# A macaron layer in split fp32: shifted weight buffers for half-size products, an out-projection in order of readiness, and a root for 1/rms

## The chip, the cores and the metric

The kernel runs on one core of a Trainium2 chip. The metric is the device time of one execution in microseconds (us); several executions of one kernel are given by their median. Matmuls run on TensorE (PE; its weight loads are a row of their own, PEld), elementwise work on VectorE (DVE) and ScalarE (ACT), some on GpSimd (POOL), and transfers are issued by queues, most by SyncE's (SP).

## The reference

One layer on x of 512 tokens by 1024 columns, all in float32:

```python
x = x + 0.5 * swiglu_ffn(rmsnorm(x, ffn1_norm), ffn1_w_gate, ffn1_w_up, ffn1_w_down)
x = x + hybrid_mixer(rmsnorm(x, mix_norm), w_in, q_norm, k_norm, rel_bias, pool_w, pool_scale, w_out)
x = x + 0.5 * swiglu_ffn(rmsnorm(x, ffn2_norm), ffn2_w_gate, ffn2_w_up, ffn2_w_down)
x = rmsnorm(x, final_norm)
```

`swiglu_ffn` is `(silu(x @ gate) * (x @ up)) @ down` with an inner width of 2816. The mixer projects to q, k, v (8 heads of 64) and to u (512 columns); heads attend to all earlier chunks and their own with a relative bias, u goes through trailing means over 2, 4, 8 and 16 tokens and a 128 by 128 map per group. Both results, side by side, go through one out-projection of 1024 by 1024. `rmsnorm` multiplies by 1/sqrt(mean(x*x) + 1e-6).

## The kernel before, in words

**Split products.** Every fp32 matrix is split into a high part (a cast by ACT) and a low part (the rest, by DVE), and a product is three matmuls (`mm3`, L162): high by high, high by low, low by high. The first operand of a matmul is the stationary one, loaded 128 by 128 by PEld; the second streams through.

**Stages.** (1) FFN 1, up: the norm, five of the 22 column blocks in plain form, then 17 blocks in a form with fewer multiplications: the operands are cut in 2 by 2 and seven products of half size are formed (here called half-size up products). For each block `product` (L519) runs seven times, each four steps of `mm3` with 256 streamed columns: 84 matmuls. The stationary operand is a weight part, the streamed one a half of the normed x (`ha`, `xa`, `sa`). (2) FFN 1, down: seven products with 512 streamed columns, in which the weights stream (`Down.product`, L740). (3) The mixer. (4) and (5): FFN 2, up and down. The final norm is folded into the end of stage 5.

**Where weight parts lie.** `part_tiles` (L145) hands out a high and a low tile of 128 by 1024 floats from four places in turn: three in the pool "weights" and one in the pool of the FFN. In the half-size products `high` (L429) takes such a pair for each of four parts of a block, `high11`, `high13`, `high24` and `high22`, always in this order, so that each kind of part always has the same place. Pools lie one behind the other in the memory, in the order in which they are made, and tiles in steps of 32 bytes. In the FFN stages every operand of these products starts at the same remainder of 512 bytes. In the mixer, the tiles `m` (q, k, attention results, pooled results) lie behind one tile `u` and two tiles `us` of 528 floats, 2112 bytes each, and so start 3 x 64 = 192 bytes off that remainder.

**1/rms.** `Norm.per_token` (L279) sums squares with 1-column matmuls and computes 1/sqrt on DVE from an integer guess and three Newton steps (`rsqrt`, L236: 11 operations, with a copy behind them). The end has its own form for one column (`rsqrt_column`, L216). Silu and Exp on ACT each need a table that a load brings in.

**The mixer's order** is written out by a planner at build time: each piece of work is a generator with a rank, and `run_parts` takes, at each simulated PE time, the ranked first one that is ready; `on` adds assumed costs. The order so found is fixed for PE, DVE, ACT and POOL. `products` (L1313) is the lowest rank: q/k, u and v projections, then the out-projection (`project_out`, L1266) in a fixed order of weight chunks: for output blocks 0 to 3 the pooled half, then the attention half by pairs of heads, then blocks 4 to 7. A chunk's product waits until its own source is there. Weights are split two chunks ahead (`next_weights`, L938).

**The end.** The last product of stage 5 is split: output rows 256 to 383 first (`tt` 0), then rows 384 to 511 in two halves of 256 columns. After each come `residual` (DVE), `settle` (squares with a sum on ACT or DVE, and a multiplication by the final gain on POOL) and `finish` (1/rms, scaling, one store of 512 KB per 128 rows).

**Loads of x.** During stage 2 each product from the fifth on issues one load of x (256 KB) on SP's queue, ahead of the next weights.

Of the kernel before, what the change touches and what calls it, by code (L numbers as in the profile page):

```python
# [16 lines left out]
P = 128  # L17
D = 1024
S = 512
# [16 lines left out]
HILO = 3  # L36
PLAIN = 5
PROBS = 3
M_TILES = 18
# [5 lines left out]
SLACK = 2.5  # L45

@with_exitstack
def layer(
# [42 lines left out]
    n_tiles = [0]  # L91

# [77 lines left out]
    def cut(pair, lo, n):  # L170
        return pair[0][:, lo : lo + n], pair[1][:, lo : lo + n]
# [14 lines left out]
    table = const.tile([P, 1], F32, name="table")  # L186
    nc.vector.memset(ones, 1.0)

    nc.scalar.copy(table, ones[:, 0:1])
# [26 lines left out]
    def rsqrt_column(v):  # L216

        half = small.tile([P, 1], F32, tag="rc", name=name("half"), bufs=8)
        y = small.tile([P, 1], F32, tag="rc", name=name("y"), bufs=8)
        neg = small.tile([P, 1], F32, tag="rc", name=name("neg"), bufs=8)  # L220
        nc.vector.tensor_scalar(
            half.bitcast(I32), v.bitcast(I32), 1, None, op0=ALU.logical_shift_right
        )
        nc.vector.tensor_scalar(neg, v, -0.5, None, op0=ALU.mult)
        nc.vector.tensor_scalar(
            y.bitcast(I32), half.bitcast(I32), -1.0, MAGIC, op0=ALU.mult, op1=ALU.add
        )
        for _ in range(3):
            b = small.tile([P, 1], F32, tag="rc", name=name("b"), bufs=8)
            z = small.tile([P, 1], F32, tag="rc", name=name("z"), bufs=8)  # L230
            nc.vector.scalar_tensor_tensor(b, y, neg, y, op0=ALU.mult, op1=ALU.mult)
            nc.vector.scalar_tensor_tensor(z, b, 1.5, y, op0=ALU.add, op1=ALU.mult)
            y = z
        return y

    def rsqrt(v, n):  # L236
# [17 lines left out]
        return y  # L254

    class Norm:
# [22 lines left out]
        def per_token(self, total):  # L279
# [5 lines left out]
            v = small.tile([P, NT], F32, tag="v", name=name("v"))  # L285
            nc.vector.tensor_scalar(v, total[:, :NT], 1.0 / D, EPS, op0=ALU.mult, op1=ALU.add)
            r = rsqrt(v, NT)
            self.r = small.tile([P, NT], F32, tag="r", name=name("r"))
            nc.vector.tensor_copy(self.r, r)
# [13 lines left out]
        def finish(self):  # L303
            self.per_token(abank())
            self.spread(abank())
# [64 lines left out]
    def ffn_up(norm, wA, down, loaded):  # L370
# [236 lines left out]
    class Down:  # L607
# [36 lines left out]
        def begin(self, pool):  # L644
            self.pool, self.acts = pool, []
            self.raws, self.parts, self.pairs = {}, {}, {}
            self.n_products, self.loads = 0, []
# [137 lines left out]
    with tc.tile_pool(name="act1", bufs=1, reuse_waits="tile") as apool:  # L785
# [4 lines left out]
        with tc.manual_schedule(engines={mybir.EngineType.SP}):  # L790
            for g in range(G):
# [53 lines left out]
    with tc.tile_pool(name="mix", bufs=1, reuse_waits="tile") as mpool:  # L845
# [16 lines left out]
        def start(part, rank):  # L862
# [36 lines left out]
        def t_act(n):  # L899
            return 0.18 + n / 1200  # L900

        def t_dve(n):
            return 0.08 + n / 930
# [24 lines left out]
        def prepare():  # L928
            i = len(ready)
            hi = wpool.tile([P, 1024], F32R, tag="hi", name=name("whi"))  # L930
            lo = wpool.tile([P, 1024], F32R, tag="lo", name=name("wlo"))
# [6 lines left out]
        def next_weights(ahead=2):  # L938
            used[0] += 1
            while len(ready) < min(used[0] + ahead, len(sources)):  # L940
                prepare()
                fetch()
            hi, lo, t = ready[used[0] - 1]
# [55 lines left out]
        def project_qk(half):  # L999
# [13 lines left out]
            start(qk_norm(half, raw), RANK_QK)  # L1013
            yield from project(acc, evacuate)

        def qk_norm(half, raw):
# [20 lines left out]
            rs = rsqrt(var.rearrange("p t h -> p (t h)"), NT * 8)  # L1037
            on("dve", 13 * 0.21)
# [67 lines left out]
        def scores(pair):  # L1106
# [7 lines left out]
            for t in range(NT - 1, -1, -1):  # L1114
# [12 lines left out]
                for i, h in enumerate(heads):  # L1127
                    start(softmax(h, t, sc[i], f), RANK_HEAD + 0.01 * h)
# [3 lines left out]
        def head(h):  # L1132
# [19 lines left out]
            for group in ((1, 3), (0,), (2,)):  # L1152
# [13 lines left out]
                start(evacuate(group, at, n, tp, on("pe", n / P * 0.11)), RANK_HEAD + 0.01 * h)  # L1166
# [48 lines left out]
        def pool():  # L1215
            for g in (3, 2, 1, 0):
# [10 lines left out]
                while step < win:  # L1227
                    yield from until(f, "pool")
                    s2 = mpool.tile([P, PAD + S], F32, tag="us", name=name("us"), bufs=2)
                    at = 2 * step - 1  # L1230
                    nc.gpsimd.tensor_tensor(
                        s2[:, at:], s[:, at:], s[:, at - step : PAD + S - step], op=ALU.add
# [6 lines left out]
                    dd, s[:, PAD:], 1.0 / win, u[:, PAD:], op0=ALU.mult, op1=ALU.subtract  # L1239
# [5 lines left out]
                start(pool_map(g, dd, on("dve", t_dve(S) + 0.4)), RANK_POOL)  # L1245
# [20 lines left out]
        def project_out(d0, part, ks, w):  # L1266

            for d in (d0, d0 + 1):
                if d not in out_acc:
                    out_acc[d] = yield from take("mm")  # L1270
            for k in ks:
                if part:
                    while 2 * k + 1 not in done:
                        yield None
                    yield from until(max(done[2 * k], done[2 * k + 1]))
                    src = aT[k]
                else:
                    while pT_out[k] is None:
                        yield None
                    src, f = pT_out[k]  # L1280
# [281 lines left out]
```

## Time and profile before

| what | us |
|---|---|
| median of 3 runs (878.69 to 879.39) | 879.09 |
| the profiled execution | 877.12 |
| its span, first to last instruction | 875.1 |
| PE busy in the span | 856.1 (98%) |
| DVE, ACT, POOL busy | 715.3, 495.7, 126.8 |
| half-size up products, FFN 1 and FFN 2 | 63.6 to 234.2, 588.6 to 758.6 |
| mixer | 346 to 528 |

A matmul's row gives its start and a duration that covers its way through the array; successive matmuls overlap. What a matmul costs in a stream is the distance from its start to the next start (called its pitch here). Where PE is busy without a break, the time of a stage is the number of matmuls times their pitch.

### The profile page before, as it was taken

What the parts mean: (1) busy time and instruction counts of PE and PEld (TensorE: products, weight loads), DVE (VectorE), ACT (ScalarE), POOL (GpSimd) and SP (SyncE); (2) the same over time, 40 slices, a digit from 0 to 9 for tenths busy, and PEclk for the clock granted to TensorE, in tenths of its full rate; (3) what the DMA queues carried; (4) which work ended last, traced back from release to release, by engine and by line L of the source; (5) the groups of instructions that cost most, each with busy time, mean ns of one, the idle gap of its engine ahead of it and who ended that gap; (6) DMA issues with size and microseconds to landing.
All of it is one profiled execution on the core that took longest, in us unless ns stands there. A gap on an engine that the chain in (4) does not pass through costs nothing.

```text
span 875.1 us, 14159 instructions
## 1 busy us (share of the span) xinstructions
PE 856.1 (98%) x5296; PEld 761.5 (87%) x5296; DVE 715.3 (82%) x1151; ACT 495.7 (57%) x841; POOL 126.8 (14%) x209
## 2 busy tenths in 40 slices
PE   9999999999999999989999999999999999999995
PEld 8789999999987888867876787889999999988885
DVE  7799888888887769686777577969888888887897
ACT  7355555555556656548747455445555555556572
POOL 0013112211122000120020000102112111122011
PEclk9999999999999999999999999999999999999998
DMA  8167778768899654222120126247777768899822
GB/s 294 44 193 215 215 226 200 187 193 212 235 326 285 217 200 143 87 85 85 72 73 25 49 97 241 97 119 221 208 228 201 187 197 206 250 326 346 275 91 96
DMA packets 71955, 158.49 MB, mean 181 GB/s; under 512 B 6080, under 2 KB 29136, under 8 KB 71504
## 3 DMA queue, kind: packets, MB, share of 16 engines
q1 hardware_dynamic: 49088, 111.45, 35.4%
q0 software_dynamic: 22656, 46.14, 24.6%
q8 instruction: 41, 0.67, 0.3%
q14 instruction: 26, 0.21, 0.1%
q10 hardware_dynamic: 144, 0.01, 0.0%
HBM read 153.38 MB, written 50.34 MB: 233 GB/s over the span
## 4 chain that ended last, share of the span: by engine, by line
PE 84%; DVE 8%; DMA 4%; ACT 2%; issue 2%; SPq 0%; POOLq 0%; POOL 0%; ACTq 0%; DVEq 0%
PE mm L166 20%; PE mm L167 20%; PE mm L168 20%; PE a L167 6%; PE a L166 6%; PE a L168 6%; DMA raw<-wsum 3%; DVE wlo L124 1%; PE a L1176 1%; PE a L1122 1%; PE a L1164 1%; ACT whi L123 1%; DVE t L1043 1%; DVE aside L324 0%; PE a L192 0%
## 5 line engine op out<-in xcount | busy, mean ns | idle before, releaser
L123 ACT CAST whi<-raw 128x1024 fp32r<-128x1024 f32 (+2 forms) x107 | 102.8, 969 | 72.0 <-PE mm L168 14.6
L124 DVE TENSOR_TENSOR wlo<-raw,whi 128x1024 fp32r<-128x1024 f32 (+2 forms) x107 | 119.5, 1121 | 23.2 <-ACT whi L123 22.6
L168 PE MATMUL mm<-ha,wlo 128*128 128x256 f32 x408 | 115.5, 283 | 0.0
L167 PE MATMUL mm<-ha,whi 128*128 128x256 f32 x408 | 115.5, 283 | 0.0
L166 PE MATMUL mm<-ha,whi 128*128 128x256 f32 x408 | 115.5, 283 | 0.0
L527 ACT ACTIVATE t<-mm 128x256 f32<-128x256 f32 x102 | 39.2, 384 | 125.5 <-PE mm L168 124.8
L436 DVE TENSOR_TENSOR wlo<-wsum,whi 128x1024 fp32r<-128x1024 f32 x68 | 83.0, 1221 | 15.1 <-ACT whi L431 15.1
L167 PEld LDWEIGHTS mm<-ha,whi 128*128 128x128 f32 x408 | 78.3, 192 | 0.1
L166 PEld LDWEIGHTS mm<-ha,whi 128*128 128x128 f32 x408 | 78.3, 192 | 0.1
L168 PEld LDWEIGHTS mm<-ha,wlo 128*128 128x128 f32 x408 | 78.3, 192 | 0.0
L166 PE MATMUL mm<-hhi,whi 128*128 128x512 f32 x192 | 76.8, 403 | 0.7 <-DVE t L382 0.7
L168 PE MATMUL mm<-hhi,wlo 128*128 128x512 f32 x192 | 74.9, 392 | 0.4 <-DVE wlo L124 0.4
L167 PE MATMUL mm<-hlo,whi 128*128 128x512 f32 x192 | 74.9, 391 | 0.0
L660 POOL COPY mark<-t 128x1 f32<-128x1 f32 x40 | 11.7, 291 | 423.3 <-DVE t L572 235.2
L662 POOL DMA_DIRECT2D wsum<-in_wB_dram x72 | 70.1, 1085 | 12.0 <-issue 9.9
L431 ACT CAST whi<-wsum 128x1024 fp32r<-128x1024 f32 x68 | 67.8, 1045 | 4.4 <-PE mm L167 3.9
L167 PE MATMUL mm<-wlo,ah 128*128 128x512 f32 x176 | 68.5, 389 | 0.0
L168 PE MATMUL mm<-whi,ah 128*128 128x512 f32 x176 | 68.5, 389 | 0.0
L166 PE MATMUL mm<-whi,ah 128*128 128x512 f32 x176 | 68.4, 389 | 0.0
L436 DVE TENSOR_TENSOR wlo<-raw,whi 128x512 fp32r<-128x512 f32 x68 | 62.2, 952 | 0.0
L431 ACT CAST whi<-raw 128x512 fp32r<-128x512 f32 x68 | 56.4, 829 | 5.5 <-PE mm L167 4.4
L167 PE MATMUL a<-wlo,ah 128*128 128x512 f32 (+1 forms) x154 | 55.8, 362 | 1.2 <-DVE wlo L124 1.2
(207 smaller groups left out, 2403.2 us busy)
## 6 DMA issues: line engine op xcount, KB each, us to landing
raw<-in_wA_dram SPq DMA_DIRECT2D x87, 512.0 KB, 5.3
wsum<-in_wB_dram POOLq DMA_DIRECT2D x60, 512.0 KB, 6.8
raw<-wsum SPq DMA_DIRECT2D x40, 512.0 KB, 6.1
raw<-in_wB_dram SPq DMA_DIRECT2D x30, 512.0 KB, 5.1
wsum<-wsum POOLq DMA_DIRECT2D x20, 512.0 KB, 5.5
x<-in_xT_dram SPq DMA_DIRECT2D x16, 256.0 KB, 6.0
raw<-in_wQK_dram SPq DMA_DIRECT2D x8, 512.0 KB, 3.5
raw<-in_wO_dram SPq DMA_DIRECT2D x8, 512.0 KB, 3.4
```

What stands on the lines that cost most here:

```text
L123: nc.scalar.copy(hi, src)
L124: nc.vector.tensor_tensor(lo, src, hi.bitcast(F32), op=ALU.subtract)
L166: nc.tensor.matmul(acc, a[0], b[0], start=start, stop=False, **more)
L167: nc.tensor.matmul(acc, a[0], b[1], start=False, stop=False, **more)
L168: nc.tensor.matmul(acc, a[1], b[0], start=False, stop=stop, **more)
L431: nc.scalar.copy(hi, src)
L436: nc.vector.tensor_tensor(lo, src, hi.bitcast(F32), op=ALU.subtract)
L527: nc.scalar.activation(dst, src, AF.Copy, scale=scale)
L660: nc.gpsimd.tensor_copy(mark, after[:, 0:1])
L662: nc.gpsimd.dma_start(self.rows(i, g), self.rows(self.terms[i][at], g), **(dict(accum_op=ALU.add) if at else {}),)
L1043: nc.vector.tensor_tensor(q3, q3, rs[:, t, :].unsqueeze(2).to_broadcast([P, 8, HD]), op=ALU.mult)
L1122: nc.tensor.matmul(sc[i][:, :n], qT[pair][0][a][rows, t * P : (t + 1) * P], kT[pair][0][b][rows, :n], start=a + b == 0, stop=a == 1,)
```

## The change

1. Weight parts lie in buffers of 1152 floats in place of 1024. In the half-size up products the part begins 16, 32, 64 or 8 floats (64, 128, 256 or 32 bytes) into its buffer, by the place; elsewhere at its start.
2. The tiles `us` of the mixer get 40 floats (160 bytes) more each, and a tile `step` of 64 bytes, which nothing uses, is put into the pool "small". The mixer has 16 tiles `m` in place of 18.
3. The out-projection is one generator which takes, among all chunks and sources that are left, the first that is ready at the simulated time; blocks 4 and 5 accumulate in the other group of PSUM banks. Four of its eight weight chunks are split into tiles of the norm's pool.
4. 1/rms of the three norms and of the end: a root on ACT, then reciprocal and one Newton step on DVE (four operations). Loads of the tables for Sqrt and Silu are placed by hand.
5. Loads of x in FFN 1's down stage begin with the 20th product in place of the 5th.
6. The end is written in a fixed order for PE, DVE and ACT: the finishing of rows 256 to 383 stands between the two halves of the last rows, the gain is multiplied on DVE, and the stores of the last two row blocks are split over ACT's and SP's queues.

```diff
-M_TILES = 18
+ROOM, STEPS = 1024 + 128, (16, 32, 64, 8)
+M_TILES = 16
...
+    small.tile([P, 16], F32, name="step", bufs=1)
...
-    def part_tiles():
+    def part_tiles(steps=(0,)):
         pool, bufs = part_rooms[n_parts[0] % len(part_rooms)]
+        at = steps[n_parts[0] % len(steps)]
         n_parts[0] += 1
         return (
-            pool.tile([P, 1024], F32R, tag=tag, name=name("w" + tag), bufs=bufs)
+            pool.tile([P, ROOM], F32R, tag=tag, name=name("w" + tag), bufs=bufs)[:, at : at + 1024]
             for tag in ("hi", "lo")
         )
...
+    def tables(func, after):
+        nc.scalar.activation(table[:, 0:1], after, func, scale=0.0)
+    tables(AF.Sqrt, ones[:, 0:1])
...
+    def rsqrt_of(v, root, out):
+        n = v.shape[-1]
+        y, a, b = (
+            small.tile([P, n], F32, tag=f"rs{n}", name=name("rs"), bufs=3) for _ in range(3)
+        )
+        nc.vector.reciprocal(y, root)
+        nc.vector.tensor_tensor(a, y, y, op=ALU.mult)
+        nc.vector.scalar_tensor_tensor(b, a, -0.5, v, op0=ALU.mult, op1=ALU.mult)
+        nc.vector.scalar_tensor_tensor(out, b, 1.5, y, op0=ALU.add, op1=ALU.mult)
...
+            nc.scalar.activation(root, total[:, :NT], AF.Sqrt, scale=1.0 / D, bias=eps)
+            if after:
+                tables(after, root[:, 0:1])
             nc.vector.tensor_scalar(v, total[:, :NT], 1.0 / D, EPS, op0=ALU.mult, op1=ALU.add)
-            r = rsqrt(v, NT)
+            rsqrt_of(v, root, self.r)
...
-            hi, lo = (z[:, : src.shape[-1]] for z in part_tiles())
+            hi, lo = (z[:, : src.shape[-1]] for z in part_tiles(STEPS))
...
+            if self.n_products == 12:
+                tables(AF.Sqrt, a[0][:, 0, 0:1].bitcast(F32))
-            if self.n_products > 4 and self.loads:
+            if self.n_products > self.loads_from and self.loads:
...
-                    down1.loads = [(x[k], xT[k]) for k in range(KD)]
+                    down1.loads, down1.loads_from = [(x[k], xT[k]) for k in range(KD)], 19
...
-                    s2 = mpool.tile([P, PAD + S], F32, tag="us", name=name("us"), bufs=2)
+                    s2 = mpool.tile([P, PAD + S + 40], F32, tag="us", name=name("us"), bufs=2)
...
+        def project_out():
+            chunks = [(0, 0), (2, 0), (0, 1), (2, 1), (4, 0), (4, 1), (6, 0), (6, 1)]
...
+            while left:
+                times = [start_at(*z) for z in left]
+                at = next((i for i, t in enumerate(times) if t is not None and t <= clock["pe"]), None)
+                if at is None:
+                    yield min((t for t in times if t is not None), default=None)
+                    continue
+                c, k = left.pop(at)
...
+                if len(left) == 16:
+                    tables(AF.Sqrt, ones[:, 0:1])
...
-            if t >= NT // 2:
-                nc.gpsimd.tensor_tensor(z, z, gb[half][:, cols], op=ALU.mult)
+            if t >= NT // 2 and half:
+                nc.vector.tensor_tensor(z, z, gb[half], op=ALU.mult)
...
+                nc.scalar.activation(o[:, S:], xt[NT + t], AF.Copy, scale=r)
+                by_vector(0)
+                nc.scalar.dma_start(rows[:, S:], o[:, S:])
+                nc.sync.dma_start(rows[:, :S], o[:, :S])
...
+        with tc.manual_schedule(engines={E.PE, E.DVE, E.Activation}):
+            for tt in range(2):
+                t = 2 + tt
+                for i, at in enumerate(p7[tt]):
+                    for g, a, w in late:
+                        down2.mms([[at]] * 2, g, a, w, (tt,), further=True)
+                    residual(0, t, *at, scale=-0.5)
+                    if i == 0 and tt:
+                        settle(0, t, 0, *at[1:])
+                        finish(t - 1, mean(t - 1, [1]), 0)
+                        v = mean(t, [1, 0])
+                    else:
+                        settle(0, t, 2 * i, *at[1:])
+            finish(t, v, 2)
```

More of the change, by code (lines that the diff above doesn't have):

```diff
@@ L213, in constants @@
         yield
[L216 to L234, printed above, removed]
     def rsqrt(v, n):
@@ L860, in on, with start @@
             return clock[engine] + HOP
-        def start(part, rank):
+        def start(part, rank, key=None):
+            rank += RANKS.get(key, 0.0)
             n_tiles[0] += 1
@@ L929, in prepare @@
             i = len(ready)
-            hi = wpool.tile([P, 1024], F32R, tag="hi", name=name("whi"))
-            lo = wpool.tile([P, 1024], F32R, tag="lo", name=name("wlo"))
+            if len(sources) - i in (3, 4, 5, 6):
+                hi, lo = (
+                    [hpool.tile([P, S], F32R, tag="h", name=name(what)) for _ in range(2)]
+                    for what in ("whi", "wlo")
+                )
+                for j in range(2):
+                    split(raws[i][:, j * S : (j + 1) * S], hi[j], lo[j])
+                    t = on("dve", t_dve(S), on("act", t_act(S)))
+                ready.append((hi, lo, t))
+                return
+            hi = wpool.tile([P, ROOM], F32R, tag="hi", name=name("whi"))[:, :1024]
+            lo = wpool.tile([P, ROOM], F32R, tag="lo", name=name("wlo"))[:, :1024]
             nc.scalar.copy(hi, raws[i])
@@ L1036, in qk_norm @@
             )
-            rs = rsqrt(var.rearrange("p t h -> p (t h)"), NT * 8)
-            on("dve", 13 * 0.21)
+            v = var.rearrange("p t h -> p (t h)")
+            if half in QK_ROOT:
+                root, rs = (
+                    small.tile([P, NT * 8], F32, tag=what, name=name(what), bufs=1)
+                    for what in ("qk_root", "qk_r")
+                )
+                f = on("dve", 0.4)
+                yield from until(f, "act")
+                nc.scalar.activation(root, v, AF.Sqrt)
+                f = on("act", 0.21)
+                yield from until(f, "dve")
+                rsqrt_of(v, root, rs)
+                on("dve", 4 * 0.21)
+            else:
+                rs = rsqrt(v, NT * 8)
+                on("dve", QK_NORM)
             rs = rs.rearrange("p (t h) -> p t h", h=8)
@@ L1264, in layer, with start_at @@
         out_acc = {}
[L1266 to L1271, printed above, removed]
-                if part:
[L1273 to L1280, printed above, removed]
-                    yield from until(f)
+        def project_out():
+            chunks = [(0, 0), (2, 0), (0, 1), (2, 1), (4, 0), (4, 1), (6, 0), (6, 1)]
+            first = len(sources) - len(chunks)
+            left = [(c, k) for c in range(8) for k in ((0, 1, 2, 3) if chunks[c][1] else (3, 2, 1, 0))]
+            n_left = dict.fromkeys(range(KD), 8)
+            begun = set()
+            def start_at(c, k):
+                d0, part = chunks[c]
+                tag = "a" if d0 == 4 else "mm"
+                if first + c >= len(ready):
+                    return None
+                if d0 not in out_acc:
+                    if len(room[tag]) < 2 or (tag == "a" and len(multiplied) < FILL_AT):
+                        return None
+                t = ready[first + c][2]
+                if d0 not in out_acc:
+                    t = max(t, sorted(room[tag])[1])
+                if part:
+                    if 2 * k + 1 not in done or 2 * k not in done:
+                        return None
+                    return max(t, done[2 * k], done[2 * k + 1])
+                return None if pT_out[k] is None else max(t, pT_out[k][1])
+            prepare_to(len(sources) - len(chunks) + AHEAD)
+            while left:
[5 more added lines that the diff above has]
+                c, k = left.pop(at)
+                d0, part = chunks[c]
+                if c not in begun:
+                    begun.add(c)
+                    prepare_to(first + len(begun) + AHEAD)
+                for d in (d0, d0 + 1):
+                    if d not in out_acc:
+                        tag = "a" if d0 == 4 else "mm"
+                        out_acc[d] = (yield from take(tag)), tag
+                src = aT[k] if part else pT_out[k][0]
@@ L1301, in finish_norm @@
         def finish_norm():
-            while used[0] < 3:
+            while used[0] < NORM_AT:
                 yield None
```

125 lines of the change are left out of this document (61 added, 64 removed).

## Prediction

> **What bounds the kernel now.** First the page: its span, busy times and chain.
>
> ```profile
> span 875.1 us, 14159 instructions
> PE 856.1 (98%) x5296; PEld 761.5 (87%) x5296; DVE 715.3 (82%) x1151; ACT 495.7 (57%) x841; POOL 126.8 (14%) x209
> PE 84%; DVE 8%; DMA 4%; ACT 2%; issue 2%; SPq 0%; POOLq 0%; POOL 0%; ACTq 0%; DVEq 0%
> ```
>
> PE is busy almost throughout and makes the chain. So two things count: the pitch of the matmuls, and the few places where PE stands still. Next the busy times by stage (stretch, its length, then busy time and count for PE, PEld, DVE, ACT, POOL):
>
> ```profile
> 63.60:234.20 170.60, 170.60 (x1422) 170.53 (x1421) 148.50 (x208) 95.07 (x172) 36.35 (x54) 1.00 0.76 201
> 346.00:528.00 182.00, 175.76 (x876) 139.25 (x875) 128.61 (x298) 105.65 (x209) 18.05 (x30) 1.00 0.22 77
> 29.00:31.00 2.00, 1.29 (x6) 0.72 (x6) 1.60 (x3) 1.98 (x3) 0.00 (x0) 1.00 0.00 0
> 279.00:285.00 6.00, 4.79 (x20) 3.35 (x19) 4.83 (x7) 3.88 (x5) 0.00 (x0) 1.00 1.03 297
> 463.00:479.00 16.00, 14.00 (x80) 10.30 (x79) 13.43 (x37) 10.92 (x26) 1.38 (x1) 1.00 0.09 34
> 500.00:504.00 4.00, 2.39 (x12) 1.74 (x11) 1.59 (x3) 0.58 (x1) 0.00 (x0) 1.00 0.00 0
> ```
>
> The half-size products of FFN 1 have no gap: 1422 matmuls in 170.60 us, a pitch of 0.120 us. 512 columns come at 0.227 in the rows below, so 256 columns take 6 ns more than half of that. Nothing but the pitch can shorten this stage. The mixer's PE is idle for 6.2 us; the four short stretches show where PE stands still.
>
> Then the matmuls one by one (start, duration), from FFN 1's down stage and from the out-projection, both with 512 streamed columns:
>
> ```profile
> 239.61 0.39 PE L168 MATMUL mm<-whi,ah 128*128 128x512 f32 x1
> ...
> 242.56 0.39 PE L166 MATMUL mm<-whi,ah 128*128 128x512 f32 x1
> ```
> ```profile
> 504.05 0.40 PE L168 MATMUL mm<-m,wlo 128*128 128x512 f32 x1
> ...
> 506.85 0.40 PE L168 MATMUL mm<-m,wlo 128*128 128x512 f32 x1
> ```
>
> The first are 13 matmuls in 2.95 us, 0.227 each; the second 12 in 2.80 us, 0.2333 each. Shape, clock and split are the same. What differs by the tile sizes is where the operands begin: in the first both at the same remainder of 512 bytes, in the second `m` lies 192 bytes off. **So the place of the operands already costs 6.6 ns per matmul in one stage.**
>
> **The change part by part.** The sum is made against the profiled execution, 877.1 us (its span and 2.0 around it); the median of the runs is 2.0 above that, and I carry these 2.0 over.
>
> *Half-size products (edit 1).* Their number is 2 FFNs x 17 blocks x 84 = 2856, at 0.120. Before, streamed and stationary operand start at the same remainder; after, the weights are shifted: `high11` comes first when ten pairs have been handed out, so by the rotation its part (12 of 84 matmuls) gets 256 bytes, `high13` 32, `high24` 64 and `high22` 128 (24 matmuls each). ACT and DVE, which write the parts, have 75 and 22 us to spare in the stage. What the shift does to the pitch at 256 columns no row shows. The nearest rows are where 256 columns run out of their rhythm, six between matmuls of 512, in the last product:
>
> ```profile
> 852.44 0.28 PE L166 MATMUL a<-whi,ah 128*128 128x256 f32 x1
> ...
> 853.15 0.40 PE L166 MATMUL a<-whi,ah 128*128 128x512 f32 x1
> ...
> 853.85 0.28 PE L166 MATMUL a<-whi,ah 128*128 128x256 f32 x1
> ```
> ```profile
> 862.21 0.28 PE L166 MATMUL a<-whi,ah 128*128 128x256 f32 x1
> 862.32 0.28 PE L167 MATMUL a<-wlo,ah 128*128 128x256 f32 x1
> 862.44 0.28 PE L168 MATMUL a<-whi,ah 128*128 128x256 f32 x1
> ...
> 864.00 0.28 PE L166 MATMUL a<-whi,ah 128*128 128x256 f32 x1
> ```
>
> Six of 256 take 0.71 us, 0.118 each, and the three of 512 behind them 0.70, 0.233 each, just what the off-remainder `m` takes. In an undisturbed row (the second fence) 256 columns begin with 0.11 and settle at 0.120. So there are two regimes: a settled one (0.227 and 0.120) and an unsettled one (0.233 and 0.118), in which 512 columns lose and 256 columns win. The out-projection rows say that a shift gives the unsettled one. Scaled by columns, 0.2333 x 256/512 = 0.1167. I take 0.1175, between 0.1167 and 0.118: -2.5 ns x 2856 = **-7.1 us**. Bounds: half of the settled 512 columns, 0.1135, for all (-18.6), and the out-projection's loss per matmul, +6.6 ns (+18.9). I choose the row with the same 256 columns over the row with the same cause, because what a matmul loses there grows with its columns.
>
> *Tiles `us` and `step` (edit 2).* u and two `us` are now 2112 + 2 x 2272 = 6656 = 13 x 512 bytes, so `m` comes to the common remainder. The small pool, counted tile by tile, stays at 4608 bytes with `step`, and the weights' six buffers add 6 x 512, so everything else keeps its remainder. 192 matmuls of the out-projection and 12 of the pool maps go from 0.2333 to 0.2267: **-1.3 us**. Bounds 0 and -1.4.
>
> *Out-projection as ready (edit 3).* The idle of 2.0 us at 463 and of 1.6 us at 500:
>
> ```profile
> 469.68 0.41 PE L1164 MATMUL a<-ident,prob 128*128 128x128 f32 x2 [0.72 <-DVE m L1191]
> ```
> ```profile
> 501.58 0.50 PE L166 MATMUL mm<-m,whi 128*128 128x512 f32 x1 [0.67 <-ACT m L1186]
> 503.02 0.50 PE L167 MATMUL mm<-m,whi 128*128 128x512 f32 x1 [0.94 <-DVE m L1191]
> ```
>
> At 501.58 PE waits for the last head's result while the pooled halves of blocks 4 to 7, which don't need it, stand behind; the new order has them. At 463 to 479 the first pairs of heads are done and could be used. The wait that may come instead is for weights: a chunk is split by ACT and DVE two chunks ahead, four of the chunks wait for the norm's tiles, free only after the last u product, and 16 tiles `m` in place of 18 must do. I take 3.0 of 3.6: **-3.0 us**. Bounds -3.6 and +2.0 (a stall as long as that at 463 once more). The stall at 375 to 384, behind the q/k norm, keeps its 11-operation root and stays.
>
> *Root (edit 4).* The first norm, and the table load behind it:
>
> ```profile
> 22.74 0.16 DVE L286 TENSOR_SCALAR v<-a 128x4 f32<-128x4 f32 x1 [0.75 <-PE a L281]
> ...
> 26.17 0.17 DVE L289 COPY r<-z 128x4 f32<-128x4 f32 x1
> ```
> ```profile
> 30.15 0.50 PE L166 MATMUL mm<-hhi,whi 128*128 128x512 f32 x1 [0.71 <-DVE t L382]
> ```
> ```profile
> L384 ACT ACT_TABLE_LOAD x2 | 2.6, 1283 | 0.0
> ```
>
> Small DVE operations follow at 0.2 us: 12 behind the first become 4 and a hop to ACT, some 1.3 us less, and the load of Silu's table (1.28) moves in front, into ACT's idle time. The evacuation for which PE waits 0.71 us at 30.15 starts earlier: **-0.7 us** (0 to -1.1). The two other norms lie under PE's work. Three more table loads (about 3.8 us of ACT) lie in stages where ACT has a third of its time free.
>
> *Loads of x (edit 5).* PE stands 1.2 us between 279 and 285, at weights that landed late, after eight loads of 256 KB went ahead on SP's queue. Now these go behind the 19th product, to about 285 to 306, where the DMA engines are as full. **-0.8 us**, bounds -1.2 and +1.2.
>
> *The end (edit 6).*
>
> ```profile
> 864.13 1.30 POOL L1392 TENSOR_TENSOR xt<-xt,t 128x512 f32<-128x512 f32 x1 [20.52 <-ACT t L1388]
> ```
> ```profile
> 864.27 1.17 DVE L1400 SCALAR_TENSOR_TENSOR v<-ssq,v 128x1 f32<-128x1 f32 x1
> ...
> 867.69 0.42 DVE L1375 SCALAR_TENSOR_TENSOR xt<-a,xt 128x256 f32<-128x256 f32 x1
> ```
> ```profile
> 870.65 0.72 ACT L1416 ACTIVATE o<-xt,z 128x512 f32<-128x512 f32 x1 [1.46 <-issue]
> ```
> ```profile
> L1411 DVE SCALAR_TENSOR_TENSOR o<-xt,z,t x4: 746/748/750, 858.4 to 861.9; 128x512 f32<-128x512 f32 x4
> ```
>
> A one-element operation lasts 1.17 us here, as long as POOL's multiplication: those go. The new order, from the first half's end at 864.2: residual 0.4 (864.6), squares 0.6, root 0.3 (865.5), four DVE operations 0.8, scaling 0.75 (867.1), two sums 0.3, the last residual 0.42 (867.8), squares 0.5, root 0.3, four operations 0.8 (869.4), scaling 0.75: 870.2 where the page has 871.4. **-1.1 us**, bounds +0.5 (the store issued by ACT in the way) and -2.0. The cost of the new order is that the last residual stands behind the finishing of the rows before.
>
> *Sum.* Without edit 1: 1.3 + 3.0 + 0.7 + 0.8 + 1.1 = 6.9. With it 14.0: 877.1 - 14.0 = 863.1, and 2.0 for the median: **865 us**.
>
> **The rivals.**
>
> *B: the shift does nothing.* The pitch is 0.120 for whichever of the four places a part lies in, and only 512-column rows have shown an influence; half of the shifts (128, 256) may be too even. Time: 879.1 - 6.9 = 872. The Trainium skill speaks for B: "SBUF — State Buffer", section "Who interferes with whom", gives PE two independent read ports, for streamed operand and weight load, and says that PE never waits on anyone. By that the place could not matter and 872 would follow; the 6.6 ns between the two 512-column rows speak against it.
>
> *C: the shift costs what it costs in the out-projection.* Place: the two half-size stages; price: 6.6 ns per matmul, however many columns. For it speaks that the cause is the same, a difference in remainders, and that all its 204 matmuls lose; against it the 256-column rows. With two of the three large kinds of parts hit (4/7 of 2856) 10.8 us: 872.2 + 10.8 = 883; with all 891. It turns the sign once the mean pitch rises by 6.9/2856 = 2.4 ns, at 37% of the matmuls.
>
> *D: the 6 ns that 256 columns take above half of 512 go,* pitch 0.1135: 872.2 - 18.6 = 854. For it: undisturbed rows of 256 begin with 0.11; against: none stays there.
>
> *E: the mixer's order gains nothing* because weights or tiles `m` come late: 3.0 us lost, A at 868.
>
> **How the numbers follow.** A (unsettled, with E inside its range of 859 to 871) 40%, B 18%, C 32% (875 to 891, mean 883), D 10%. The range from 853 to 885 leaves out about half of D, a quarter of C and the ends of A, 16% in all. About 0.2% (1.8 us) is what a measurement of this kernel can tell from no change. Faster: A, D, 17 of B and 6 of C, 73%; within: 1 of B and 5 of C, 6%; slower: 21 of C.
>
> **What would show it.** The pitch in the half-size stages, separately by part: 0.1175 for A, 0.120 for B, 0.1266 for C, 0.1135 for D; the stage lasts 167, 170.6, up to 180, or 161.5 us. In the out-projection 0.2267. No idle at 500, little at 463. A last scaling that begins 3.5 us after PE's last matmul in place of 4.7. The forecast is wrong if the half-size pitch rises, or if the parts differ in sign.

## The result and the profile after

The changed kernel takes **868.23 us** (median of 4 runs, 865.23 to 869.31) where the kernel before takes 879.24 beside it (878.69 to 879.93): a ratio of 0.9859, with a 95% interval from 0.9824 to 0.9894. The forecast was 865. The profiled execution took 867.31 us, 9.8 less than the one of before.

The page of the changed kernel, its span, busy times and chain:

```profile
span 865.4 us, 14127 instructions
PE 849.9 (98%) x5296; PEld 755.9 (87%) x5296; DVE 708.1 (82%) x1115; ACT 500.9 (58%) x859; POOL 126.9 (15%) x204
PE 89%; DMA 3%; DVE 3%; ACT 2%; issue 1%; SPq 0%; ACTq 0%; DVEq 0%
```

PE has the same 5296 matmuls and is still the bound. Busy time by stage after (stretch, its length, then busy time and count for PE, PEld, DVE, ACT, POOL, granted clock, DMA share, GB/s), and of before the down stage of FFN 1 and the mixer whole:

```profile
62.20:231.60 169.40, 169.40 (x1428) 169.40 (x1427) 148.56 (x207) 95.26 (x172) 36.33 (x54) 1.00 0.78 204
231.70:342.40 110.70, 108.85 (x482) 87.61 (x480) 87.11 (x114) 69.83 (x99) 14.78 (x16) 1.00 0.80 239
342.40:522.00 179.60, 175.17 (x886) 140.24 (x885) 130.21 (x297) 107.65 (x217) 18.06 (x30) 1.00 0.24 80
582.10:751.60 169.50, 169.50 (x1429) 169.49 (x1428) 148.73 (x208) 95.61 (x173) 33.28 (x54) 1.00 0.75 205
463.00:479.00 16.00, 15.92 (x90) 12.72 (x90) 15.42 (x35) 10.40 (x24) 1.38 (x1) 1.00 0.29 100
```
```profile
235.10:343.70 108.60, 107.39 (x480) 87.76 (x480) 87.35 (x114) 68.03 (x97) 12.28 (x16) 1.00 0.79 244
343.80:528.10 184.30, 178.06 (x887) 141.03 (x886) 130.91 (x300) 105.65 (x209) 18.05 (x30) 1.00 0.22 78
```

From these stretches and the starts of the matmuls at their borders, with the differences against before:

| stage | before | after | difference | forecast |
|---|---|---|---|---|
| FFN 1 up: norm and plain blocks | 63.6 | 62.2 | -1.4 | -0.7 |
| FFN 1 and 2: half-size products | 171.5, 171.4 | 169.6, 169.6 | -3.7 | -7.1 |
| FFN 1 down | 108.7 | 110.7 | **+2.0** | -0.8 |
| mixer | 184.3 | 179.6 | -4.7 | -4.3 |
| FFN 2 up: transposes, norm, plain blocks | 60.5 | 60.1 | -0.4 | 0 |
| FFN 2 down | 106.0 | 106.0 | 0 | 0 |
| behind PE's last matmul | 9.1 | 7.7 | -1.4 | -1.1 |

Two terms are off: the shift of the weight parts gave half of what was expected, and FFN 1's down stage got longer. The stages are those of one traced execution each; the times of the changed kernel's four executions differ by 4.1 us.

One block of half-size products in FFN 2: the first matmul of each of its seven products of 12, and of the next block (start, duration).

```profile
612.03 0.28 PE L176 MATMUL mm<-ha,whi 128*128 128x256 f32 x1
...
613.46 0.28 PE L176 MATMUL a<-xa,whi 128*128 128x256 f32 x1
...
614.88 0.28 PE L176 MATMUL mm<-xa,whi 128*128 128x256 f32 x1
...
616.29 0.28 PE L176 MATMUL a<-ha,whi 128*128 128x256 f32 x1
...
617.70 0.28 PE L176 MATMUL mm<-ha,whi 128*128 128x256 f32 x1
...
619.12 0.28 PE L176 MATMUL mm<-ha,whi 128*128 128x256 f32 x1
...
620.56 0.28 PE L176 MATMUL mm<-sa,whi 128*128 128x256 f32 x1
...
622.00 0.28 PE L176 MATMUL mm<-ha,whi 128*128 128x256 f32 x1
```

The distances are 1.43, 1.42, 1.41, 1.41, 1.42, 1.44, 1.44 us. By the place of the weights these are the parts with 256, 32, 64, 64, 32, 128 and 128 bytes. Over all blocks the mean pitch is 119.0 ns (256 bytes), 118.3 (32), 117.8 (64) and **120.0 (128: nothing gained)**, against 120.0 before. With 12, 24, 24 and 24 matmuls of a block: 12 x 1.0 + 24 x 1.7 + 24 x 2.2 = 106 ns, times 34 blocks = 3.6 us.

The other steps, in rows of after: two matmuls of the out-projection, 34 pitches apart; first and last DVE operation of the first 1/rms; PE's last matmul and the last scaling.

```profile
502.98 0.39 PE L176 MATMUL mm<-m,whi 128*128 128x512 f32 x1
...
510.69 0.39 PE L177 MATMUL a<-m,whi 128*128 128x512 f32 x1
```
```profile
23.32 0.16 DVE L301 TENSOR_SCALAR v<-a 128x4 f32<-128x4 f32 x1 [0.30 <-ACT root L298]
...
23.99 0.16 DVE L264 SCALAR_TENSOR_TENSOR r<-rs,rs 128x4 f32<-128x4 f32 x1
```
```profile
857.36 0.28 PE L178 MATMUL a<-whi,ah 128*128 128x256 f32 x1
...
860.81 0.72 ACT L1496 ACTIVATE o<-xt,r 128x512 f32<-128x512 f32 x1 [0.81 <-DVE r L264]
```

7.71 us over 34 is 0.2268, so the tiles `m` run at the short pitch. The root's chain ends at 24.15 where the copy of before ended at 26.34. In before, a weight split of 1.23 us stood in the middle of that chain on DVE:

```profile
24.44 1.23 DVE L124 TENSOR_TENSOR wlo<-raw,whi 128x1024 fp32r<-128x1024 f32 x1
```

In after nothing stands between its operations.

The last scaling begins 3.2 us behind the end of PE's last matmul (857.64), 4.7 before.

### The profile page after: what moved, and what is told of

It is laid out like the page before. It is cut to its first block, busy times and chain, and to the rows that moved or that the text cites. A ratio compares the mean times of both kernels' runs of the same rounds, so it can differ in the third digit from the quotient of the medians.

```text
span 865.4 us, 14127 instructions
## 1 busy us (share of the span) xinstructions
PE 849.9 (98%) x5296; PEld 755.9 (87%) x5296; DVE 708.1 (82%) x1115; ACT 500.9 (58%) x859; POOL 126.9 (15%) x204
## 4 chain that ended last, share of the span: by engine, by line
PE 89%; DMA 3%; DVE 3%; ACT 2%; issue 1%; SPq 0%; ACTq 0%; DVEq 0%
PE mm L176 21%; PE mm L177 21%; PE mm L178 21%; PE a L177 7%; PE a L178 7%; PE a L176 7%; DMA raw<-wsum 2%; PE a L1167 1%; DMA raw<-in_wB_dram 1%; PE a L1221 1%; PE a L1209 1%; DVE wlo L132 1%; DMA raw<-in_wA_dram 1%; DVE t L1088 1%; ACT prob L1148 1%
## 5 line engine op out<-in xcount | busy, mean ns | idle before, releaser
L132 DVE TENSOR_TENSOR wlo<-raw,whi 128x1024 fp32r<-128x1024 f32 (+2 forms) x115 | 125.3, 1096 | 28.7 <-ACT whi L131 28.4
L131 ACT CAST whi<-raw 128x1024 fp32r<-128x1024 f32 (+2 forms) x115 | 107.3, 944 | 67.8 <-PE mm L177 15.5
L176 PEld LDWEIGHTS mm<-ha,whi 128*128 128x128 f32 x408 | 77.2, 189 | 0.1
L177 PEld LDWEIGHTS mm<-ha,whi 128*128 128x128 f32 x408 | 77.1, 189 | 0.1
L673 POOL COPY mark<-t 128x1 f32<-128x1 f32 x40 | 14.9, 373 | 409.1 <-DVE t L585 231.1
```

Of the source, the lines that this page charges most:

```text
L132: nc.vector.tensor_tensor(lo, src, hi.bitcast(F32), op=ALU.subtract)
L176: nc.tensor.matmul(acc, a[0], b[0], start=start, stop=False, **more)
L177: nc.tensor.matmul(acc, a[0], b[1], start=False, stop=False, **more)
L673: nc.gpsimd.tensor_copy(mark, after[:, 0:1])
```

## The experiments

Times are medians; beside them, on the same chip, the kernel before took 877.8 to 878.8 us. Stages and pitches are read from one traced execution of each kernel. Except in the two kernels of matmul rows, every edit is to the changed kernel, here called after.

### Does the place set the pitch: rows of matmuls alone

```diff
+for n, d in ((n, d) for n in (256, 512) for d in (0, 4, 8, 12, 16, 24, ... 124)):
+    for i in ...:                       # rows of 60 (256 columns) or 48 (512 columns)
+        matmul(acc, whi[:, d + k * 128 : ...], xhi[:, at : at + n])
+        matmul(acc, whi[:, d + k * 128 : ...], xlo[:, at : at + n])
+        matmul(acc, wlo[:, d + k * 128 : ...], xhi[:, at : at + n])
```

> This kernel leaves the layer out: it only runs rows of matmuls in split form (high by high, high by low, low by high, 60 of 256 or 48 of 512 streamed columns per row) with the stationary operand shifted by 0 to 124 floats against the common remainder of 512 bytes, and PE has no other load. Theory (two regimes, set by the difference of remainders): at 256 columns 0.120 us without shift and 0.117 to 0.119 with 8, 16 or 64 floats; at 512 columns 0.227 without shift and about 0.233 with most shifts. Rival 1 (the loss is per matmul): a shift that costs 512 columns 6 ns costs 256 columns the same. Rival 2 (the place is of no matter, other traffic makes the difference): every row of a width has the same pitch. Three rows more shift the streamed operand alone (16, 64 floats) or both by 16: the theory, which knows only the difference, wants 0.117 to 0.119 in the first two and 0.120 in the last.

The first matmul of three successive rows of 60, whose stationary operand lies 16, 24 and 32 floats off (the number stands behind the o in the name), and the borders of the row of 48 with 512 columns at 16 floats:

```profile
37.72 0.28 PE L53 MATMUL m256o16x<-xhi,whi 128*128 128x256 f32 x1
...
44.53 0.28 PE L53 MATMUL m256o24x<-xhi,whi 128*128 128x256 f32 x1
...
51.74 0.28 PE L53 MATMUL m256o32x<-xhi,whi 128*128 128x256 f32 x1
...
152.67 0.39 PE L53 MATMUL m512o16x<-xhi,whi 128*128 128x512 f32 x1
...
163.86 0.39 PE L53 MATMUL m512o24x<-xhi,whi 128*128 128x512 f32 x1
```

With 16 floats the row of 60 takes 6.81 us, with 24 it takes 7.21. The program changes nothing else between them but the accumulator, which takes four buffers of PSUM in turn and was not varied by itself; in the layer, below, the shift alone is changed. The pitch once a row is in its rhythm (mean over its last 44 or 32 distances):

| shift, bytes | 0 | 32 | 48 | 64 | 96 | 128 | 192 | 256 | 320 | 448 | 496 |
|---|---|---|---|---|---|---|---|---|---|---|---|
| 256 columns, ns | 120.0 | 118.5 | 123.3 | **113.3** | 120.0 | 118.6 | 117.8 | 120.0 | 117.8 | 117.8 | 117.3 |
| 512 columns, ns | 226.7 | 233.3 | 233.3 | 233.3 | 234.3 | 232.6 | 228.9 | 226.7 | 233.3 | 228.8 | 226.7 |

With the streamed operand shifted by 64 bytes in place of the stationary one it is 117.8, as at 448 (64 short of 512); with both shifted by 64 it is 120.0, as without shift. So it is the difference of the two places that matters, with no other engine at work on these operands. That the shift does nothing falls, and so does a loss per matmul that is the same for 256 columns as for 512: at 64 bytes the one wins 6.7 ns and the other loses 6.6. But the theory of two regimes falls too: it wanted 0.117 to 0.119 at 64 and 256 bytes, where 113.3 and 120.0 came. Nor do 256 columns always win: at 48 bytes both widths lose. And the layer is not the rows: there 128 bytes gave 120.0 and 256 bytes 119.0.

### Without the shift

```diff
-ROOM, STEPS = 1024 + 128, (16, 32, 64, 8)
+ROOM, STEPS = 1024 + 128, (0, 0, 0, 0)
```

> The changed kernel with all four shifts zero, buffers as large as there. Theory: the half-size products go back to 0.120 us, each of the two stages from 169.55 to about 171.4 us, so 3.7 us more than the changed kernel, 871 to 872 by the medians. Rival (the shorter half-size stages come from the earlier 1/rms or other edits): the stages stay at 169.5 and the time within 1 us of the changed kernel.

871.64 us, ratio 0.9914 (0.9885 to 0.9943). Both half-size stages by windows:

```profile
62.50:233.80 171.30, 171.30 (x1429) 171.30 (x1428) 148.69 (x208) 95.37 (x173) 36.28 (x54) 1.00 0.77 202
584.80:756.00 171.20, 171.20 (x1429) 171.20 (x1428) 148.66 (x208) 95.50 (x173) 33.17 (x54) 1.00 0.75 203
```

Taken from the border matmuls both stages last 171.35 again, 1.8 more each than in after: the shift is worth 3.6 us, and all other parts together the rest of the gain. The stages show this; in the whole time the two intervals overlap.

### 64 bytes in all four places

```diff
+ROOM, STEPS = 1024 + 128, (16, 16, 16, 16)
```

> The changed kernel with 64 bytes in all four places. In its trace the part with 64 bytes ran at 0.1177 us, those with 32, 256 and 128 bytes at 0.1183, 0.1190 and 0.1201. Theory (the shift of a place alone sets its pitch): all parts come to 0.1177, each stage to about 168.1 us, 2.8 us less in sum: about 865.4. Rival (it is the alternation of different shifts, or what is multiplied, that makes the difference): the parts keep their own pitches and the stages stay at 169.5, or go back to 171.4.

859.76 us, ratio 0.979 (0.9767 to 0.9814).

```profile
62.20:230.30 168.10, 168.10 (x1429) 168.10 (x1428) 148.57 (x208) 95.18 (x172) 36.26 (x54) 1.00 0.78 205
581.20:743.00 161.80, 161.80 (x1429) 161.80 (x1428) 147.89 (x207) 95.22 (x172) 33.39 (x54) 1.00 0.78 211
```

The same code with the same places runs at 0.1178 in FFN 1 (168.2 us for 1428 matmuls) and at 0.1134 in FFN 2 (162.0). Clock and DMA share are the same. So one place has more than one pitch, and the theory that the shift alone sets it holds for FFN 1 only. The six executions lie within 1.7 us of each other, less than the 6.2 between the two stages, so none seems to have chosen otherwise.

The two stages do not begin differently. The first matmul in FFN 2, the 25th (first of the third product) and the 49th:

```profile
581.14 0.28 PE L176 MATMUL mm<-ha,whi 128*128 128x256 f32 x1
...
583.97 0.28 PE L176 MATMUL mm<-xa,whi 128*128 128x256 f32 x1
...
586.69 0.28 PE L176 MATMUL mm<-ha,whi 128*128 128x256 f32 x1
```

The first 24 take 2.83 us, 118 ns each as in FFN 1; the next 24 take 2.72, 113.3 each, and so it stays to the end. The change comes with the 25th matmul, without a recorded wait. What brings it here and not in FFN 1 no run shows.

### What decides between the two pitches

```diff
+runs = 0, 0, 13, 14, ... 118 floats, each once; then rows of 512 columns before 16, 16, 17, 18, 20, 15;
+then 0, 16, 32, 16, 48, 16; then both operands shifted: 48 and 32, 80 and 64
```

> This kernel leaves the layer out, as the first table of pitches did: rows of 60 matmuls of 256 streamed columns with the stationary operand shifted by 13 to 118 floats, some of them straight behind a row of 48 with 512 columns, and with 16 floats behind rows of other shifts. Theory of two steady rhythms for one shift: 16 floats gave 0.1133 us by itself and in FFN 2, but 0.1177 in FFN 1, so what ran before decides which rhythm a row falls into; then 16 floats shows both values here, by its predecessor. Rival (the rhythm follows from the shift alone, and FFN 1 has other traffic): 16 floats gives 0.1133 each time. Neighbours (13 to 20 floats): 0.1133 for multiples of 4 bytes close by if it is the difference in 64-byte lines that counts, about 0.118 if only 16 fits. The last two rows shift both operands, by 48 and 32, and by 80 and 64: 0.1133 if only the difference counts.

Rows at 16 floats (64 bytes), twice in the same kernel, each with the start of the row behind it:

```profile
45.38 0.28 PE L55 MATMUL m256o16x0r<-xhi,whi 128*128 128x256 f32 x1
...
52.45 0.28 PE L55 MATMUL m256o17x0r<-xhi,whi 128*128 128x256 f32 x1
...
267.26 0.28 PE L55 MATMUL m256o16x0r<-xhi,whi 128*128 128x256 f32 x1
...
274.07 0.28 PE L55 MATMUL m256o32x0r<-xhi,whi 128*128 128x256 f32 x1
```

7.07 us the first time, 6.81 the second: 117.8 and 113.3 per matmul. Both are steady (118, 118, 117, 119, 117 over and over, and 113, 113, 114). The row at 64 bytes ran short behind a row without shift and behind one of 192 bytes (and of 48, in the first kernel); long behind 60 bytes, behind 128, and both times straight behind 512 columns. With both operands shifted, 64 bytes apart, it was long once and short once. So a place has at least two rhythms, and which one a row falls into goes with what ran before, though each predecessor but the 512 columns was tried once only. In the layer the half-size stages follow 512 columns and began long with 64 bytes, as here; that FFN 2 then changed is not explained by it. 52 bytes (13 floats) and 76 bytes (19) gave the short one the only time each was tried; of the other shifts none did.

### 76 and 52 bytes in all four places

```diff
+ROOM, STEPS = 1024 + 128, (19, 19, 19, 19)      # the other kernel: (13, 13, 13, 13)
-                    down1.loads, down1.loads_from = [(x[k], xT[k]) for k in range(KD)], 19
+                    down1.loads, down1.loads_from = [(x[k], xT[k]) for k in range(KD)], 4
```

> Kernel after with all four places of the weight parts 76 bytes (19 floats) into their buffers, and the loads of x from the 5th product. In the rows of matmuls alone 19 floats gave 0.1133 (seen once). Theory (the place decides which rhythms there are, and at 19 floats the short one is entered easily): both half-size stages at 0.1133, 161.9 us each; against the kernel with 64 bytes everywhere (859.8; 168.2 and 162.0) only the first stage wins, 6.2: 853.5 us. Rival 1 (what runs just before the stage decides, and FFN 1's stage has the wrong start): first stage 168.2, second 162.0: 859.5 us. Rival 2 (at 19 floats the long rhythm, 0.1177, in both): 168.2 each, 866 us. Rival 3 (the rows alone don't carry over to this place): 171.4 each, 871.6 us.

> Kernel after with all four places of the weight parts 52 bytes (13 floats) into their buffers, and the loads of x from the 5th product. In the rows of matmuls alone 13 floats gave 0.1133 after an unsettled start. Theory: both half-size stages near 0.1133, 161.9 us each, 853.5 us. Rival 1 (the start decides, not the place): 168.2 and 162.0, 859.5 us. Rival 2 (the long rhythm in both): 168.2 each, 866 us. Rival 3 (this place is neutral in the layer): 171.4 each, 871.6 us.

76 bytes: **852.07 us** (849.98 to 854.43), ratio 0.9703 (0.9677 to 0.9729): the fastest kernel of this study. 52 bytes: 869.17, ratio 0.9887 (0.9843 to 0.9931). Both half-size stages of each by windows, 76 bytes first:

```profile
62.00:223.90 161.90, 161.90 (x1429) 161.89 (x1428) 147.92 (x207) 95.37 (x172) 37.39 (x54) 1.00 0.81 210
572.90:734.80 161.90, 161.90 (x1429) 161.88 (x1428) 148.08 (x207) 95.31 (x172) 33.46 (x54) 1.00 0.77 211
```
```profile
63.00:234.20 171.20, 171.20 (x1429) 171.20 (x1428) 148.51 (x208) 95.72 (x173) 36.35 (x54) 1.00 0.77 202
585.10:756.30 171.20, 171.20 (x1429) 171.20 (x1428) 148.58 (x208) 95.64 (x173) 33.32 (x54) 1.00 0.74 203
```

At 76 bytes both stages hold the short rhythm to the end: 162.0 us each, 7.6 less than in after, as the theory had it. They are in it from the fourth matmul on, and return to it within nine after a hesitation of some 0.09 us at the 25th. At 52 bytes, which had the short rhythm in the rows alone, the layer has the mean pitch of no shift, 171.4 each (rival 3), in a rhythm of its own (120, 118, 122 ns over and over, where no shift has 120 each time). So rows alone show that the pitches exist; which one a place gets in the layer has to be tried there. Why 52 bytes are long in the layer stays open. The trace is of the slowest of four executions, 863.0 to 872.4 us, the widest spread of these kernels; whether both stages were long in the other three is not shown.

### The mixer: order and place of `m`

```diff
-            yield from project_out()              # as ready
+            ...                                   # the fixed order of before, all in banks "mm"
```

> The changed kernel with the out-projection in the fixed order of the kernel before; the load of Sqrt's table stands ahead of blocks 4 to 7. Theory (the order fills PE's idle time): of the 4.74 us by which the mixer became shorter, 1.3 belong to the place of the tiles m and about 3.4 to the order, so the mixer goes from 179.6 to about 183.0 us. Rival (the mixer's gain comes from the place of m and from the shorter norm): it stays below 180.5.

```diff
-                    s2 = mpool.tile([P, PAD + S + 40], F32, tag="us", name=name("us"), bufs=2)
+                    s2 = mpool.tile([P, PAD + S], F32, tag="us", name=name("us"), bufs=2)
```

> The changed kernel with tiles us of 528 floats again, so that m and what lies behind it start 192 bytes off the common remainder. Theory: 192 matmuls of the out-projection and 12 of the pool maps go from 0.227 to about 0.233 us, the mixer from 179.6 to about 180.9 us. Rival (the loss at the off remainder is hidden by waits in the mixer): 179.6 as before.

Fixed order: 873.27 us, ratio 0.9932 (0.9909 to 0.9955). `m` off the remainder: 867.98, ratio 0.9876 (0.9848 to 0.9904), which in the whole time can't be told from after. The mixer of each by windows, then waits of PE in the mixer (who waited for what: us in total, times, longest): two of the fixed order that after doesn't have, and two of after:

```profile
341.80:525.10 183.30, 177.00 (x887) 141.04 (x886) 129.81 (x296) 107.70 (x217) 18.07 (x30) 1.00 0.24 79
```
```profile
341.80:522.20 180.40, 176.11 (x886) 140.28 (x885) 130.20 (x296) 107.61 (x217) 18.06 (x30) 1.00 0.24 80
```
```profile
PE mm L177 <- DVE m L1236: 1.0, 1, 1.0
...
PE mm L176 <- ACT m L1231: 0.7, 1, 0.7
```
```profile
PE a L1209 <- DVE m L1236: 1.1, 1, 1.1
PE a L1209 <- ACT prob L1148: 0.6, 1, 0.6
```

The order is worth 3.7 us of the mixer (183.3 against 179.6). The waits of the out-projection for the last head's `m`, 1.0 and 0.7, are back with the fixed order; those behind the q/k norm and at u are in both kernels. But the new order has waits of its own, 1.1 and 0.6, at 488 to 491 us, for results of the attention. PE's idle time differs by only 1.9 us (183.3 - 177.0 against 179.6 - 175.2). The other 1.8 is less busy time for the same matmuls. An estimate of its cause: a matmul in front of a wait counts 0.39 us as busy, in a stream 0.227, and after has fewer waits. The place of `m` is worth 0.9 (180.5 by the borders): its matmuls are back at 0.233. That is less than the 1.3 of the theory; where the rest went is not shown. Together 4.5 of the 4.7 that the mixer won.

### FFN 1's down stage: table, loads of x

```diff
-                    down1.loads, down1.loads_from = [(x[k], xT[k]) for k in range(KD)], 19
+                    down1.loads, down1.loads_from = [(x[k], xT[k]) for k in range(KD)], 4
...
-            if self.n_products == 12:
+            if self.n_products == (30 if self is down1 else 12):
...
+        with tc.manual_schedule(engines={mybir.EngineType.SP}):
             for g in range(G):
                 if g + 1 < G:
                     down1.product(p7, g + 1, S3, T3)
                 down1.product(p5, g, S4, B22, further=True)
```

The first kernel has the first edit, the second the first two (the table for Sqrt comes later), the third only the last (SP's order by hand in the second loop of products too).

> The changed kernel with the loads of x begun behind the fourth product again. In the trace of the changed kernel these loads, meant for the 20th product on, are issued at 232 to 243 us, before those of the kernel before (235 to 251, counted from a start 3.3 us later), because only the first loop fixes the order of SP's queue. Theory: this crowding costs the 2.0 us by which FFN 1's down stage became longer; undone, the stage goes from 110.7 to about 108.7 us and the time down by 2. Rival 1 (the load of Sqrt's table at the twelfth product, 1.28 us on ACT, is the cause) and rival 2 (the stage now starts earlier than its sums of weights are ready): the stage stays at 110 to 111 us.

> The changed kernel with the loads of x behind the fourth product, as in loads4, and the load of Sqrt's table in FFN 1's down stage at the 30th product in place of the 12th. loads4 brought the stage from 110.7 to 109.65 us, the kernel before has 108.7. Theory: the remaining 1.0 us is the table load, 1.28 us on ACT among splits that PE waits for: 108.7. Rival (the stage is held by transfers that vary from run to run): 109.5 to 111.

> Kernel after with SP's order written by hand in the second loop of products of FFN 1's down stage too, so that the eight loads of x really go out between the weights of the 20th to the 27th product, and not in front of them. Theory (the order on the queue holds weights up): the weights of the second loop come first, the down stage takes 0.8 us less than in the kernel before, 107.9 us in place of 110.7: 865.5 us. Rival (the volume of the transfers in that stretch holds PE, whatever their order): 109.5 to 111.5 us, 868 us, with idle of PE only moved.

When the loads of x were issued (count, shortest, median and longest issue in ns, first and last start): before, after, and with SP's order by hand.

```profile
L745 SPq DMA_DIRECT2D x<-in_xT_dram x8: 377/483/517, 235.4 to 251.5; - x8
```
```profile
L760 SPq DMA_DIRECT2D x<-in_xT_dram x8: 327/432/1262, 224.7 to 240.3; - x8
```
```profile
L760 SPq DMA_DIRECT2D x<-in_xT_dram x8: 383/460/1259, 269.6 to 289.9; - x8
```

In after the loads are not later but 11 us earlier: three go out before the stage begins at 231.7 (the 232 to 243 in the first expectation left these out). In the code the order on SP's queue is written out only in the first loop of products, and the loads belong to the second; the scheduler put them ahead. Times: loads from the 5th product 865.3 us (ratio 0.9856, 0.9829 to 0.9884), with the table late too 867.0 (0.986, 0.9835 to 0.9885), loads really late 866.69 (0.9865, 0.985 to 0.9879): none can be told from after. The stage in their profiles, table late and loads really late, and behind it 3.4 us of the former; then PE's waits in this stage before and after:

```profile
231.70:345.70 114.00, 109.68 (x483) 88.97 (x481) 87.14 (x114) 69.44 (x99) 12.51 (x16) 0.99 0.79 232
```
```profile
232.40:341.70 109.30, 107.78 (x482) 87.87 (x481) 87.01 (x114) 69.55 (x99) 14.07 (x16) 1.00 0.82 242
```
```profile
282.40:285.80 3.40, 3.38 (x8) 2.71 (x9) 3.40 (x5) 1.91 (x3) 0.00 (x0) 0.50 0.62 193
```
```profile
PE a L167 <- DVE wlo L124: 1.2, 2, 0.7
```
```profile
PE a L177 <- DVE wlo L132: 1.3, 2, 0.8
PE mm L177 <- DVE wlo L132: 0.5, 2, 0.3
```

Moving the table away did not shorten the stage: it was the longest of all. Two accidents lengthen it there. One is a wait of 2.3 us for a weight part, which ACT could write only when a transfer landed late. The other is the clock: behind that wait the granted clock was 0.50 for 3.4 us, and matmuls came 427 ns apart in place of 227, some 1.6 us lost in all. The same fall of the clock, for as long, is in this stage of two more traces, that without the shift and that of 52 bytes. Why it came no run shows.

Loads that are really late give 109.3, 1.4 less than after and not the 107.9 of the theory. With loads from the 5th product, between the weights as before, four kernels show 109.3, 109.7, 111.1 and (table late) 114.0, and with the early loads of after five show 110.0 to 111.2. Without the three traces with the lower clock, 109.3 and 109.7 stand against 110.0 to 111.2. That points to the early loads as the cause of about 1 us. But these are two traces against four, and in the whole time nothing can be told; so the 2.0 us are **not settled**, and every changed kernel lies above the 108.7 of before's one profile.

What the traces do show is that PE's waits for weight parts do not go away. In all traces but that of 76 bytes they come 43 to 53 us into the stage: whether the loads went out 0 to 16 us into it (before, 1.2 us of waits), 7 us ahead of it to 9 us into it (after, 1.5 of its 1.8) or 37 to 57 us into it (really late, 1.5).

## Why the prediction came out as it did

**Half-size products, -3.7 in place of -7.1.** Right was that the place changes the pitch, and the sign. The term was mis-sized in the step "I take 0.1175" for all 2856 matmuls: only the part with 64 bytes comes near that (117.8), and the 24 of 84 with 128 bytes run at 120.0. The text itself had the warning, in rival B: "half of the shifts (128, 256) may be too even". The picture of one settled and one unsettled regime, in which 512 columns lose and 256 win, was wrong: 117.8 is a rhythm as steady as 120.0, places differ, and 64 bytes have two. So the sign is in part luck: in rows alone 48 bytes, which the change doesn't use, cost 256 columns 3.3 ns.

**B, the shift does nothing (872).** The kernel without the shift takes 871.64, so B had the price right, and the 3.6 us of the two stages are the shift. By the Trainium skill ("SBUF — State Buffer", section "Who interferes with whom") PE's two read ports are independent and PE never waits on anyone. The conclusion that B drew from this, that the place can't matter, doesn't agree with the rows of matmuls alone: 113.3 to 123.3 ns at the same shape and clock, by the distance of the two operands. Where in PE the time goes no row shows.

**C, a loss of 6.6 ns per matmul.** It falls: no part of the half-size products rose above 120.0. The nearest row with the same cause had 512 columns, that with the same columns another cause; choosing the second came out right for these four shifts.

**D, pitch 0.1135 (854).** Not what the change does, but it exists: 0.1133, half of 0.2267, held in one stage with 64 bytes everywhere and in both with 76. "None stays there" was true only of the rows of before.

**Loads of x, +2.0 in place of -0.8.** The failed step is "now these go behind the 19th product, to about 285 to 306". It took the place in the code for the place in the queue; the trace has them at 224.7 to 240.3. The same sentence says that the DMA engines are as full there, which is misread: before has a DMA share of 0.64 from 290 to 310 us, 1.06 from 240 to 260. And its premise, that eight loads ahead on the queue make PE wait at 279 to 285, isn't borne out: with the loads really late PE still waits 1.5 us there. What of the 2.0 comes from the early loads stays open, as above.

**The mixer, -4.7 for -4.3.** Right in sum: 3.7 for the order where 3.0 stood, 0.9 for the place of `m` where 1.3 stood. The idle at 500 is gone, and at 463 to 479 PE is busy for 15.92 of 16.00. E falls. But "I take 3.0 of 3.6" counted idle time, and 1.7 us of it came back at 488 to 491, for attention results and not for weights as the text feared. That PE's busy time fell by as much was not in the sum, so that the size fits is in part luck.

**Root and end.** -1.4 for -0.7: the chain on DVE ended 2.2 us earlier, not 1.3, and no row of PE waits at 30 us any more. The prediction counted 0.2 us for each operation and overlooked the weight split of 1.23 us that stood among them. The length of this stage varies from 61.9 to 62.9 between the changed kernels, so the difference is good to half a microsecond. The end gave -1.4 for -1.1, by the order forecast.

In sum, against the profiled 867.3 where 863.1 was worked out: 3.4 too much from the shift and 2.8 from the loads, less 2.0 too little from the other terms. So the total lies nearer to 865 than its two largest misses because others went the other way.

## What to carry to other kernels

Where PE streams without a break, measure the pitch and compare it with that of other shapes: here 256 columns cost 6 ns more than half of 512, and moving the weights by 76 bytes took that away, 18.7 us in the two stages together (2 x (171.35 - 162.0)). Try such a place in the kernel itself and read the pitch in each stage, since the same place can run at two pitches. Look at the granted clock of a stage, too, before its length is put down to an edit. And read from the trace when a transfer is issued: where the order of a queue isn't written out, its place in the code doesn't tell.

## What was not expected of the hardware

- In these rows a stream of matmuls of one shape had steady rhythms of 113.3 to 123.3 ns (256 columns) and 226.7 to 234.3 ns (512), by the distance of its two operands in memory, at a granted clock of 1.00.
- At one distance (64 bytes) there were two, 117.8 and 113.3 ns. In rows alone it went with what ran before. In the layer one stage kept the first for 1428 matmuls (168.2 us), and the other changed to the second after 24 (162.0 us).
- The best of these places for 256 columns (64 bytes: 113.3) was bad for 512 (233.3 against 226.7).
- In three traces the granted clock fell to 0.5 for some 3.4 us in the middle of the layer, and matmuls of 512 columns came 427 ns apart in place of 227.
- Shorter half-size stages were in part given back: with 64 and 76 bytes everywhere FFN 2's down stage lasted 107.4 and 107.2 us in place of 106.0. In each of the two PE waited once for a weight part that DVE had not yet written, 1.0 and 0.8 us; in after no such wait is recorded there.
